# A hybrid encoder layer on one core: equal matmul widths side by side, W cleared in pieces, two heads' inverses sent apart

## The chip, the core and the metric

The kernel runs on one core of a Trainium2 chip. TensorE (PE) does the matmuls, VectorE (DVE) and ScalarE (ACT) the elementwise work, GpSimd (POOL) clears memory and issues part of the DMAs, SyncE (SP) issues the others. The metric is the device time of one execution in microseconds; before the change its median over three runs is 2288.46 us (2286.44 to 2289.66).

## The reference, cut to what matters

Two sequences of 256 tokens (width 2048) go through one encoder layer and a last RMSNorm. All arithmetic is float32.

```
proj  = rmsnorm(h) @ w_in
y_na  = neighbourhood_attention(q, k, v, rpb)         # 8 heads; 4 rows of 64 columns, windows of 16 columns
y_dn  = gated_deltanet_bidir(qkv, z, b, a, ...)       # 8 heads; forwards and backwards, chunks of 64 tokens
h     = h + concat(y_na, y_dn) @ w_out
hn    = rmsnorm(h)
h     = h + (silu(hn @ w_gate) * (hn @ w_up)) @ w_down
# within a chunk of the delta rule:
a_mat = strict lower part of (k_beta @ k.T) * decay
t_mat = inverse of (I + a_mat)                        # triangular, 64 x 64
u = t_mat @ v_beta;  w = t_mat @ (k_beta * exp(g));  then a recurrence over 4 chunks
```

## The kernel before

Every float32 product is made of products in the fp32r format. A weight tile of 128x1024 is split by `split` (L135, L136): ACT writes its rounded part `w_hi`, DVE the remainder `w_lo`. Activations are kept as such pairs too.

The stages, by time in the trace:

- To about 230 us: the q and k column tiles of the delta-rule heads (`col_tile`, each two `half_gemm` of 24 matmuls, 512 columns wide), the convolution, Gram matrices sent to DRAM (`s_gram`).
- 230 to 520 us: the q, k, v tiles of the eight attention heads; beside them runs `attend` (L615) as a generator that `pump` advances between matmuls. At the same time `lanes` (L477) inverts all 128 chunk matrices at once, one per partition, on DVE: `W` (128 partitions x 64 x 64, in the buffer that held the decays `E`) is cleared by one POOL memset (L552), then filled column by column (L562, L564); `half_gemm` advances this generator once per half tile. The results are written over `kkq` (L574 for partitions 0 to 63, L577 for 64 to 127) and sent to DRAM (`s_uq`, L582) by eight DMAs of 16 partitions on POOL's queue.
- 520 to 780 us: v and z tiles of the delta-rule heads, and beside them the recurrence. `open_recurrence` opens the pool `dr` in the memory that `lanes` gave back, clears the four buffers `uq` (L703) and `prepare` reads the inverses of a head back from `s_uq` (L720, four DMAs a head, POOL's queue). The matmul that needs them is `ps_s<-dvn,uq`.
- 780 to 950 us: the output projection (`w_out`).
- 950 to 1815 us: gate and up. 44 calls of `block` compute a 2x2 block product with seven products instead of eight (sums of weights come from accumulating DMAs and DVE). 1858 to 2177 us: 16 such blocks of the down projection, in two groups of eight; the rest of it (`down`, `down_half`) is plain.

One call of `product` (L985) is 8 matmuls of 512 columns with `w_hi` (7 in the down groups), then 8 (7) of 256 columns with `w_lo`. The scheduler keeps the matmuls in the order of the program. Other engines' instructions are ordered by a planner from priorities (`tc.high_priority`) and due times; each engine then runs its instructions in that order. Weight splits go through three buffers each for `hi` and `lo`.

In `attend`, the score rows `na_s` (tags `s0`, `s1`) hold probabilities and zeros outside the window: each head takes new tiles and POOL clears the outside (L636); the output `na_o` takes the buffer `s0` and is sent to `s_na` by POOL's queue (L674).

Of the kernel before, what the change touches and what calls it, by code (L numbers as in the profile page):

```python
# [18 lines left out]
P = 128  # L19
# [36 lines left out]
FIN_GAP = 5  # L56

LANE_WORK = 1800
HALF, BAND = 32, 40

WARM = 56
# [10 lines left out]
def hybrid_encoder(ctx: ExitStack, tc: tile.TileContext, xT, w_in, w_ba, w_out, w_gate,  # L72
# [50 lines left out]
    s_qq = dp.tile([4, H, NB, C], F32, name="s_qq")  # L123
    s_kq = dp.tile([H, P, 2, T], F32, name="s_kq")
    s_gram = dp.tile([4, H * NB, C, 2, C], F32, name="s_gram")
    s_uq = dp.tile([H * NB, 2, C, 4, 2, C], F32, name="s_uq")
    s_na = dp.tile([H, P, T], F32, name="s_na")
    s_h1 = dp.tile([KT, P, T], F32, name="s_h1")
    s_h2 = dp.tile([KT, P, T], F32, name="s_h2")
# [338 lines left out]
    def decays(s0, s1):  # L468

        G, NG, E = gt["G"], gt["NG"], gt["E"]  # L470
        for s in range(s0, s1):
# [2 lines left out]
            pin(act(out=E[half[1], s, :s + 1], in_=G[half[1], :s + 1], func=AF.Exp,  # L474
                    bias=NG[half[1], s:s + 1]))

    def lanes():  # L477
        beta, kd, eg, dg, E = (gt[n] for n in ("beta", "kd", "eg", "dg", "E"))
        qq = vec("qq")

        gram = s_gram.rearrange("k n s w c -> (k n) s (w c)")
        quarters = [slice(q * 16, q * 16 + 16) for q in range(4)]
        for sl in quarters:
            nc.gpsimd.dma_start(kkq[half[0], sl].rearrange("p s w c -> p s (w c)"), gram[:, sl])
        for d in range(2):
            nc.gpsimd.dma_start(qq[half[d]], s_qq.rearrange("k h b t -> (k h b) t"))
        yield from pause(LANE_START)
        for q, sl in enumerate(quarters):
            pin(nc.scalar.copy(kkq[half[1], sl], kkq[half[0], sl]))
            if q % 2:  # L490
                yield


        def norms(src, nm):
            x, s, r = vec(nm + "x"), vec(nm + "s"), vec(nm + "r")
            pin(ts(x, src, EPS, None, ALU.add))
            newton_rsqrt(r, x, ln)
            tt(s, x, r, ALU.mult)
            return s, r

        dgk = kkq.rearrange("p s w c -> p (s w c)")[:, 0:C * 2 * C:2 * C + 1]
        nk, rk = norms(dgk, "nk")
        _, rq = norms(qq, "nq")
        yield
        rqd = vec("rqd", 2 * C)
        for i in range(2):
            ts(rqd[:, i * C:i * C + C], rq, QSCALE, None, ALU.mult)
        egd = vec("egd", 4 * C)
        for i in range(2):
            stt(egd[:, i * C:i * C + C], eg, -1.0, rk, ALU.mult, ALU.mult)  # L510
            nc.vector.tensor_copy(egd[:, (2 + i) * C:(3 + i) * C], eg)
        Dm, ndm, rb = vec("Dm"), vec("ndm"), vec("rb")
        tt(rb, rk, beta, ALU.mult)
        tt(Dm, rk, rb, ALU.mult)
        ts(ndm, Dm, -1.0, None, ALU.mult)
        yield

        LN = {(0, 0): 0, (0, 1): 16, (0, 2): 64 + 16, (0, 3): 64,
              (1, 0): 64 + 48, (1, 1): 64 + 32, (1, 2): 32, (1, 3): 48}
        for q in range(2):  # L520
            sl = slice(q * 32, q * 32 + 32)
            tt(kkq[:, sl, 1], kkq[:, sl, 1], E[:, sl], ALU.mult)
            yield

        h0, h1 = half
        Et = E[h0].rearrange("p s c -> p c s")
        for q in range(4):
            sl = slice(q * 16, q * 16 + 16)
            n = q * 16 + 16
            tt(kkq[h0, sl, 0, :n], kkq[h0, sl, 0, :n], Et[:, sl, :n], ALU.mult)  # L530
            tt(kkq[h1, sl, 0, :n], kkq[h1, sl, 0, :n], E[h1, sl, :n], ALU.mult)
            tt(kkq[:, sl, 0, :n], kkq[:, sl, 0, :n], ndm[:, sl, None].broadcast_to([P, 16, n]),
               ALU.mult)
            yield
        ps = sm_tile()
        mm(ps[:, :P], ones, dg, start=True, stop=True)
        nc.scalar.copy(egl, ps[:, :P])
        ps = sm_tile()
        for i, v in enumerate((kd, egd[:, :2 * C], egd[:, 2 * C:], rqd)):
            transpose(ps[:, i * P:i * P + P], v, ident)  # L540
        p3 = ps[:, :3 * P].rearrange("p (i l) -> p i l", i=3)
        for (hf, st), l0 in LN.items():
            nc.scalar.copy(tab[half[hf], :, st], p3[half[hf], :, l0:l0 + 16])
        for hf in range(2):
            for pp in range(2):
                l0 = 3 * P + POS[pp][hf] * 16
                nc.scalar.copy(rqs[half[hf], pp], ps[half[hf], l0:l0 + 16])
        yield

        W = ln.tile([P, C, C], F32, tag="E", name="W")  # L550
        Wf = W.rearrange("p s c -> p (s c)")
        nc.gpsimd.memset(W, 0.0)  # L552
        nc.vector.memset(Wf[half[0], 0:C * C:C + 1], 1.0)
        nc.vector.tensor_copy(Wf[half[1], 0:C * C:C + 1], Dm[half[1]])
        work = 0
        for c in range(1, C):
            for s0 in range(0, c, BLK):
                s1 = min(s0 + BLK, c)
                n, j = s1 - s0, c - s0
                pr = ln.tile([P, BLK * C], F32, tag="prod", bufs=2, name="prod")  # L560
                pv = pr[:, :n * j].rearrange("p (s j) -> p s j", j=j)
                tt(pv, W[:, s0:s1, s0:c], kkq[:, c, 0, None, s0:c].broadcast_to([P, n, j]),  # L562
                   ALU.mult)
                nc.vector.tensor_reduce(W[:, s0:s1, c], pv, AX.X, ALU.add)  # L564
                work += 2 * n * j + 200
            if work > LANE_WORK:
                work = 0
                yield

        for d in range(2):  # L570
            for q in range(2):
                sl = slice(q * 32, q * 32 + 32)
                if d == 0:
                    tt(kkq[h0, sl, 0], W[h0, sl], rb[h0, sl, None].broadcast_to([64, 32, C]),  # L574
                       ALU.mult)
                else:
                    tt(kkq[h1, sl, 0], W[h1, :, sl].rearrange("p s c -> p c s"),  # L577
                       nk[h1, sl, None].broadcast_to([64, 32, C]), ALU.mult)
                yield
            for (hf, st), l0 in LN.items():  # L580
                if l0 // 64 == d:
                    nc.gpsimd.dma_start(  # L582
                        s_uq[:, hf, :, st].rearrange("n s w c -> n s (w c)"),
                        kkq[l0:l0 + 16].rearrange("p s w c -> p s (w c)"))

    for h in range(H):
        kq = wk.tile([P, 2, T], F32, tag="kq", bufs=2, name="kq")
# [24 lines left out]
    def part(s, c0, shift, n):  # L612
# [2 lines left out]
        return bass.AP(a.tensor, a.offset,  # L615
                       [a.ap[0], (L + shift * (C - BAND if shift > 0 else BAND), 2), (C, 4), (1, n)])

    def attend(h, qT, kT, v):

        bias = na.tile([P, 2, 4 * BAND], F32, tag="bias", bufs=2, name="bias")  # L620
# [9 lines left out]
                   by_rows(kT, b)[:, :, k0:k0 + BAND], start=True, stop=True)  # L630
        sc = []
        for b in range(NB):
            full = na.tile([P, 2, L], F32, tag=f"s{b}", name="na_s")
            sc.append(full)
            s = part(full, 0, 1, BAND)
            nc.gpsimd.memset(part(full, BAND, -1, C - BAND), 0.0)  # L636
            tt(s, pq[b][:, :8 * BAND].rearrange("p (q r c) -> p q r c", q=2, r=4),
               bias.rearrange("p q (r c) -> p q r c", r=4), ALU.add)
            mx = na.tile([P, 2], F32, tag="mx", bufs=2, name="mx")
# [24 lines left out]
            nc.scalar.copy(t, pt.rearrange("p (q k) -> p q k", q=2))  # L664
            pT.append(t)
        yield from pause(PV_GAP)
        no = na.tile([P, T], F32, tag="s0", name="na_o")
        po = sm_tile()
        for b in range(NB):
            for kt in range(2):  # L670
                mm(po[:, b * L:b * L + L], vn[:, b * 2 + kt], pT[b][:, kt],
                   start=(kt == 0), stop=(kt == 1))
        nc.scalar.copy(no, po)
        nc.gpsimd.dma_start(s_na[h], no)  # L674

    for h in range(H):
        ps = col_tile(w_in[16 + 3 * h], xs)
# [29 lines left out]

    prepared, outputs, gate, traced, finished = {}, {}, {}, set(), set()

    def prepare(h, vT):  # L710

        dr, UQ = state["dr"], state["UQ"]
        while h > 1 and not {h - 2, h - 2 ^ 1} <= traced:
            yield
        uq = UQ[2 * (h % 2):2 * (h % 2) + 2]
        kq = wk.tile([P, 2, T], F32, tag="kq", bufs=2, name="kq2")
        nc.sync.dma_start(kq, s_kq[h])
        for b in range(NB):
            for hf in range(2):
                nc.gpsimd.dma_start(  # L720
                    uq[b][half[hf], :, :, hf * C:hf * C + C].rearrange("s i w c -> s (i w) c"),
                    s_uq[h * NB + b, hf].rearrange("s i w c -> s (i w) c"))
        yield from pause(2 + h % 2)
        pv, pk = sm_tile(), sm_tile()
        for t, u in ((pv, vT), (pk, kq[:, 0])):
# [140 lines left out]
    for h in range(0, H, 2):  # L866
        vT = []
        for i in range(2):
            if h + i == 1:
                while vector_work:  # L870
                    advance(vector_work)
            while h and h + i - 2 not in prepared:
                pump()
            ps = col_tile(w_in[40 + 2 * (h + i)], xs)
# [107 lines left out]

    def product(ps, w, xc, c, first, done=False):  # L985

        wh, wl = w
        for k, x in enumerate(xc):
            mm(ps, wh[:, k], x[:, c], start=(first and k == 0), stop=False,
               skip_group_check=True)  # L990
        for k, x in enumerate(xc):
            mm(ps[:, 0], wl[:, k], x[:, c, 0], start=False, stop=(done and k == len(xc) - 1),
               skip_group_check=True)

    def plus_both(out, a, ps, op=ALU.add):
# [33 lines left out]
    def block(w4, sums, xc, ix, p1_pool, new_out, opened=None, lead=False):  # L1029
# [15 lines left out]
        pc, pd = bank(psm, "s", "ps_c"), bank(pso, "o1", "ps_d")  # L1045
        with ahead():
            w = w_split(b11)
        product(pa, w, xc, ix[A11], True)
        if lead:
            pe = bank(psm, "s", "ps_e")  # L1050
            with ahead():
                w = w_split(b21)
            product(pe, w, xc, ix[A12], True, True)
        if opened:
            opened()
        fp, out = state["fp"], new_out()
# [3 lines left out]
            plus_both(out[:, 0], p1, pe)  # L1060
        with ahead():
            w = w_split(second)
        product(pc, w, xc, ix[S3], True)
        p7 = fp.tile([P, 2, L], F32, tag="p7", name="p7")
        nc.scalar.copy(p7, pc)
        with ahead():
# [321 lines left out]
```

## Time and profile before

The median is 2288.46 us. The profiled execution took 2286.66 us by the device's own clock, its span is 2284.9 us.

| engine | busy us | share of the span | instructions |
|---|---|---|---|
| PE | 2251.9 | 99% | 12318 |
| DVE | 1760.5 | 77% | 2691 |
| ACT | 1058.2 | 46% | 1637 |
| POOL | 246.2 | 11% | 358 |

The granted TensorE clock is 0.997 of full speed over the span. A matmul row shows when it began and how long it took with its drain, which overlaps the next one; so the pace of the matmuls is read from one start to the next, not from their durations, and a PE that is 99% busy can still have slack in its pace. In a row of the timeline stand start, duration, engine, line, operation, output<-inputs, shapes, count and, in brackets, the engine's idle time before it and what ended it.

### The profile page before, as it was taken

The numbers are of one execution on the slowest core, as the hardware profiler recorded it, in microseconds if no ns is written. First come the engines' busy times: TensorE is split into PE (matmuls) and PEld (weight loads), VectorE is DVE, ScalarE is ACT, GpSimd is POOL, SyncE is SP. The second block draws the span as 40 slices with busy tenths as digits, with TensorE's granted clock in tenths as the row PEclk, the third lists the DMA queues.
The fourth block names the chain that finished last, engine by engine and source line by source line (L and its number), as shares of the span: only waits on it lengthen the run. The fifth ranks groups of instructions, "written<-read, shape, count | busy, mean of one in ns | idle before, by whom it ended". The sixth has DMA issues, their size and how long they took to land.

```text
span 2284.9 us, 32561 instructions
## 1 busy us (share of the span) xinstructions
PE 2251.9 (99%) x12318; PEld 1920.3 (84%) x12318; DVE 1760.5 (77%) x2691; ACT 1058.2 (46%) x1637; POOL 246.2 (11%) x358
## 2 busy tenths in 40 slices
PE   9999999999999999999999999999999999999998
PEld 7887788887888888888888888888888878888887
DVE  7754699983555545888888888888888788888866
ACT  6777332324333324654444444444444454444435
POOL 2211100011000010111111010101010011011110
PEclk9999999999999999999999999999999999999999
DMA  5333423245333454776777677777777477667672
GB/s 203 128 127 126 129 84 104 95 125 148 109 98 107 176 175 166 218 204 183 216 199 206 193 213 202 205 198 205 197 187 202 143 209 200 173 189 210 182 203 84
DMA packets 112316, 383.95 MB, mean 168 GB/s; under 512 B 14080, under 2 KB 14416, under 8 KB 111904
## 3 DMA queue, kind: packets, MB, share of 16 engines
q1 hardware_dynamic: 77264, 267.17, 33.5%
q0 software_dynamic: 34896, 114.71, 23.8%
q8 instruction: 97, 1.59, 0.3%
q14 instruction: 59, 0.48, 0.1%
HBM read 346.41 MB, written 35.41 MB: 167 GB/s over the span
## 4 chain that ended last, share of the span: by engine, by line
PE 83%; DVE 7%; ACT 4%; issue 3%; DMA 2%; POOL 0%; SPq 0%; DVEq 0%; ACTq 0%; POOLq 0%
PE ps_g L84 28%; PE ps_c L84 14%; PE ps_d L84 14%; PE ps_a L84 14%; PE ps_b L84 7%; PE ps_s L84 6%; DVE w_lo L136 2%; ACT w_hi L135 1%; DVE cacc L351 1%; ACT E L472 1%; ACT E L474 1%; PE ps_o L84 1%; PE ps_s L87 1%; DMA kkq<-s_gram 1%; DVE W L564 0%
## 5 line engine op out<-in xcount | busy, mean ns | idle before, releaser
L84 PE MATMUL ps_g<-xhi,w_hi 128*128 128x512 f32 x896 | 359.0, 401 | 2.7 <-DVE on L442 1.4
L84 PE MATMUL ps_g<-xhi,w_lo 128*128 128x512 f32 x896 | 351.4, 392 | 5.7 <-DVE w_lo L136 5.7
L84 PE MATMUL ps_g<-xlo,w_hi 128*128 128x512 f32 x896 | 350.2, 391 | 0.5 <-DVE xlo L255 0.5
L135 ACT ACTIVATE w_hi<-w_first 128x1024 fp32r<-128x1024 f32 (+1 forms) x180 | 185.7, 1032 | 285.9 <-PE ps_c L84 157.2
L136 DVE TENSOR_TENSOR w_lo<-w_raw,w_hi 128x1024 fp32r<-128x1024 f32 x166 | 202.4, 1220 | 133.1 <-ACT w_hi L135 132.7
L135 ACT ACTIVATE w_hi<-b 128x1024 fp32r<-128x1024 f32 (+1 forms) x180 | 185.7, 1032 | 227.9 <-issue 122.6
L135 ACT ACTIVATE w_hi<-w_raw 128x1024 fp32r<-128x1024 f32 x166 | 174.3, 1055 | 243.2 <-PE ps_g L84 201.8
L136 DVE TENSOR_TENSOR w_lo<-w_first,w_hi 128x1024 fp32r<-128x1024 f32 (+1 forms) x180 | 213.4, 1185 | 50.4 <-ACT w_hi L135 45.6
L136 DVE TENSOR_TENSOR w_lo<-b,w_hi 128x1024 fp32r<-128x1024 f32 (+1 forms) x180 | 212.7, 1182 | 3.8 <-ACT w_hi L135 3.2
L84 PEld LDWEIGHTS ps_g<-xhi,w_lo 128*128 128x128 f32 x896 | 168.7, 188 | 44.5 <-DVE w_lo L136 8.4
L84 PEld LDWEIGHTS ps_g<-xhi,w_hi 128*128 128x128 f32 x896 | 168.8, 188 | 39.9 <-issue 4.5
L84 PEld LDWEIGHTS ps_g<-xlo,w_hi 128*128 128x128 f32 x896 | 168.9, 188 | 35.1 <-DVE xlo L255 1.5
L84 PE MATMUL ps_c<-xc,w_hi 128*128 128x512 f32 x704 | 176.3, 392 | 0.0
L84 PE MATMUL ps_d<-xc,w_hi 128*128 128x512 f32 x704 | 176.3, 392 | 0.0
L84 PE MATMUL ps_a<-xc,w_hi 128*128 128x512 f32 x696 | 174.2, 392 | 0.0
L84 PEld LDWEIGHTS ps_c<-xc,w_hi 128*128 128x128 f32 x704 | 126.6, 189 | 22.6
L84 PEld LDWEIGHTS ps_d<-xc,w_hi 128*128 128x128 f32 x704 | 126.6, 189 | 22.6
L84 PEld LDWEIGHTS ps_a<-xc,w_hi 128*128 128x128 f32 x696 | 125.2, 189 | 22.4
L135 ACT ACTIVATE w_hi<-w_second 128x1024 fp32r<-128x1024 f32 (+1 forms) x60 | 61.9, 1032 | 94.4 <-PE ps_d L84 85.5
L84 PEld LDWEIGHTS ps_d<-xc,w_lo 128*128 128x128 f32 x704 | 96.0, 190 | 6.9
L84 PEld LDWEIGHTS ps_c<-xc,w_lo 128*128 128x128 f32 x704 | 96.0, 190 | 6.9
L84 PEld LDWEIGHTS ps_a<-xc,w_lo 128*128 128x128 f32 x696 | 94.9, 190 | 6.8
(374 smaller groups left out, 4223.0 us busy)
## 6 DMA issues: line engine op xcount, KB each, us to landing
w_raw<-in_w_in_dram SPq DMA_DIRECT2D x110, 512.0 KB, 3.2
b<-in_w_gate_dram SPq DMA_DIRECT2D x66, 512.0 KB, 3.9
b<-in_w_up_dram SPq DMA_DIRECT2D x66, 512.0 KB, 4.7
b<-in_w_group_dram SPq DMA_DIRECT2D x48, 448.0 KB, 4.1
w_raw<-in_w_out_dram SPq DMA_DIRECT2D x32, 512.0 KB, 3.4
w_raw<-in_w_down_dram SPq DMA_DIRECT2D x24, 512.0 KB, 3.4
w_second<-in_w_gate_dram SPq DMA_DIRECT2D x22, 512.0 KB, 7.4
w_first<-in_w_gate_dram SPq DMA_DIRECT2D x22, 512.0 KB, 5.8
```

The costliest lines, as they stand in the source:

```text
L84: pin(nc.tensor.matmul(*a, **k))
L87: pin(nc.tensor.transpose(*a))
L135: act(out=hi, in_=src, func=AF.Copy)
L136: tt(lo, src, r32(hi), ALU.subtract)
L351: stt(a3[:, :, lo:hi], x3[:, :, lo + o:hi + o], cw[:, ct, j:j + 1], a3[:, :, lo:hi], ALU.mult, ALU.add)
L472: pin(act(out=E[half[0], s, s:], in_=G[half[0], s:], func=AF.Exp, bias=NG[half[0], s:s + 1]))
L474: pin(act(out=E[half[1], s, :s + 1], in_=G[half[1], :s + 1], func=AF.Exp, bias=NG[half[1], s:s + 1]))
```

## The change

- `product` writes wide matmuls first and narrow ones second in one call, and the other way round in the next, so that runs of equal width adjoin across calls; `plain` (the leading block of a stage) starts the count anew with wide first. The flag that begins an accumulation moves to the first matmul of the call, whichever it is.
- `W` is cleared by eight memsets that cover, for each group of eight rows, only the columns up to the diagonal block: 2304 of 4096 elements per partition.
- The two probability tiles are taken once, and their outside is cleared once. `na_o` takes the buffer `vT` and is sent by ACT's DMA queue.
- `s_uq` becomes two DRAM tiles: one for heads 0 and 1 (4 of each group of 16 lanes), one for heads 2 to 7 (12). `send_lanes` sends the first part as soon as each half of the inverses is done, the second part after both: 16 DMAs instead of 8, the same bytes.
- The remaining vector work is drained, the recurrence memory opened and the fetch for heads 0 and 1 (`fetch`) issued before the first v tile, where before the drain stood before the second v tile, and opening and fetch after it.

In the built program PE's instructions stand in the old order up to the first leading block, SP's up to the second down group. On POOL's queue the clears of `uq` and the fetch follow directly behind the 16 pieces of `s_uq`; the sends of `na_o` no longer stand between them. On ACT and DVE some instructions of `attend` and of the blocks change places with weight splits.

```diff
+OPEN_AT = 0
-    s_uq = dp.tile([H * NB, 2, C, 4, 2, C], F32, name="s_uq")
+    s_uq = [dp.tile([n, 2, C, 4, 2, C], F32, name=f"s_uq{n}") for n in (4, 12)]
...
+    def send_lanes(part, d):
+        n0, n1 = ((0, 4), (4, 16))[part]
+        for (hf, st), l0 in LN.items():
+            if l0 // 64 == d:
+                nc.gpsimd.dma_start(
+                    s_uq[part][:, hf, :, st].rearrange("n s w c -> n s (w c)"),
+                    kkq[l0 + n0:l0 + n1].rearrange("p s w c -> p s (w c)"))
...
-        nc.gpsimd.memset(W, 0.0)
+        for s in range(0, C, 8):
+            nc.gpsimd.memset(W[:, s:s + 8, :s + 8], 0.0)
...
-            for (hf, st), l0 in LN.items():
-                if l0 // 64 == d:
-                    nc.gpsimd.dma_start(
-                        s_uq[:, hf, :, st].rearrange("n s w c -> n s (w c)"),
-                        kkq[l0:l0 + 16].rearrange("p s w c -> p s (w c)"))
+            send_lanes(0, d)
+        send_lanes(1, 0)
+        send_lanes(1, 1)
...
-            full = na.tile([P, 2, L], F32, tag=f"s{b}", name="na_s")
-            sc.append(full)
-            s = part(full, 0, 1, BAND)
-            nc.gpsimd.memset(part(full, BAND, -1, C - BAND), 0.0)
+            if b not in probs:
+                probs[b] = na.tile([P, 2, L], F32, tag=f"s{b}", name="na_s")
+                nc.gpsimd.memset(part(probs[b], BAND, -1, C - BAND), 0.0)
+            sc.append(probs[b])
+            s = part(probs[b], 0, 1, BAND)
...
-        no = na.tile([P, T], F32, tag="s0", name="na_o")
+        no = na.tile([P, T], F32, tag="vT", name="na_o")
...
-        nc.gpsimd.dma_start(s_na[h], no)
+        nc.scalar.dma_start(s_na[h], no)
...
+    def fetch(h):
+        uq = state["UQ"][2 * (h % 2):2 * (h % 2) + 2]
+        kq = wk.tile([P, 2, T], F32, tag="kq", bufs=2, name="kq2")
+        nc.sync.dma_start(kq, s_kq[h])
+        for b in range(NB):
+            for hf in range(2):
+                nc.gpsimd.dma_start(
+                    uq[b][half[hf], :, :, hf * C:hf * C + C].rearrange("s i w c -> s (i w) c"),
+                    s_uq[h > 1][(h * NB + b) - 4 * (h > 1), hf].rearrange("s i w c -> s (i w) c"))
+        fetched[h] = uq, kq
...
     def prepare(h, vT):
...
+        if h not in fetched:
+            fetch(h)
+        uq, kq = fetched[h]
...
-            if h + i == 1:
+            if h + i == OPEN_AT:
                 while vector_work:
                     advance(vector_work)
+                open_recurrence()
+                fetch(0)
+                fetch(1)
...
-    def product(ps, w, xc, c, first, done=False):
+    def product(ps, w, xc, c, first, done=False, plain=False):
         wh, wl = w
-        for k, x in enumerate(xc):
-            mm(ps, wh[:, k], x[:, c], start=(first and k == 0), stop=False,
-               skip_group_check=True)
-        for k, x in enumerate(xc):
-            mm(ps[:, 0], wl[:, k], x[:, c, 0], start=False, stop=(done and k == len(xc) - 1),
+        n = len(xc)
+        wide = [(ps, wh[:, k], x[:, c]) for k, x in enumerate(xc)]
+        narrow = [(ps[:, 0], wl[:, k], x[:, c, 0]) for k, x in enumerate(xc)]
+        if plain:
+            order[0] = 0
+        work = narrow + wide if order[0] % 2 else wide + narrow
+        order[0] += 1
+        for m, (out, w, x) in enumerate(work):
+            mm(out, w, x, start=(first and m == 0), stop=(done and m == 2 * n - 1),
                skip_group_check=True)
...
-        product(pa, w, xc, ix[A11], True)
+        product(pa, w, xc, ix[A11], True, plain=lead)
...
-            product(pe, w, xc, ix[A12], True, True)
+            product(pe, w, xc, ix[A12], True, True, plain=True)
...
-        product(pc, w, xc, ix[S3], True)
+        product(pc, w, xc, ix[S3], True, plain=lead)
```

More of the change, by code (lines that the diff above doesn't have):

```diff
@@ L475, in decays @@
                     bias=NG[half[1], s:s + 1]))
+    LN = {(0, 0): 0, (0, 1): 16, (0, 2): 64 + 16, (0, 3): 64,
+          (1, 0): 64 + 48, (1, 1): 64 + 32, (1, 2): 32, (1, 3): 48}
+    def send_lanes(part, d):
[5 more added lines that the diff above has]
+                    kkq[l0 + n0:l0 + n1].rearrange("p s w c -> p s (w c)"))
     def lanes():
@@ L516, in lanes @@
         yield
-        LN = {(0, 0): 0, (0, 1): 16, (0, 2): 64 + 16, (0, 3): 64,
-              (1, 0): 64 + 48, (1, 1): 64 + 32, (1, 2): 32, (1, 3): 48}
         for q in range(2):
@@ L616, in part @@
                        [a.ap[0], (L + shift * (C - BAND if shift > 0 else BAND), 2), (C, 4), (1, n)])
+    probs = {}
     def attend(h, qT, kT, v):
@@ L708, in hybrid_encoder @@
     prepared, outputs, gate, traced, finished = {}, {}, {}, set(), set()
[L710 to L715, printed above, removed]
+    fetched = {}
+    def fetch(h):
+        uq = state["UQ"][2 * (h % 2):2 * (h % 2) + 2]
         kq = wk.tile([P, 2, T], F32, tag="kq", bufs=2, name="kq2")
@@ L721, in prepare @@
                     uq[b][half[hf], :, :, hf * C:hf * C + C].rearrange("s i w c -> s (i w) c"),
-                    s_uq[h * NB + b, hf].rearrange("s i w c -> s (i w) c"))
+                    s_uq[h > 1][(h * NB + b) - 4 * (h > 1), hf].rearrange("s i w c -> s (i w) c"))
+        fetched[h] = uq, kq
+    def prepare(h, vT):
+        dr = state["dr"]
+        while h > 1 and not {h - 2, h - 2 ^ 1} <= traced:
+            yield
+        if h not in fetched:
+            fetch(h)
+        uq, kq = fetched[h]
         yield from pause(2 + h % 2)
@@ L980, in hybrid_encoder @@
             tt(acc, acc, sq, ALU.add)
-    def product(ps, w, xc, c, first, done=False):
+    order = [0]
+    def product(ps, w, xc, c, first, done=False, plain=False):
         wh, wl = w
-        for k, x in enumerate(xc):
-            mm(ps, wh[:, k], x[:, c], start=(first and k == 0), stop=False,
-               skip_group_check=True)
-        for k, x in enumerate(xc):
-            mm(ps[:, 0], wl[:, k], x[:, c, 0], start=False, stop=(done and k == len(xc) - 1),
+        n = len(xc)
[7 more added lines that the diff above has]
+            mm(out, w, x, start=(first and m == 0), stop=(done and m == 2 * n - 1),
                skip_group_check=True)
```

## Prediction

> **What bounds the kernel now.** I read the page's busy shares and chain first, then the waits of PE, then the timeline at the places that the change touches.
>
> ```profile
> span 2284.9 us, 32561 instructions
> PE 2251.9 (99%) x12318; PEld 1920.3 (84%) x12318; DVE 1760.5 (77%) x2691; ACT 1058.2 (46%) x1637; POOL 246.2 (11%) x358
> PE 83%; DVE 7%; ACT 4%; issue 3%; DMA 2%; POOL 0%; SPq 0%; DVEq 0%; ACTq 0%; POOLq 0%
> PE ps_g L84 <- DVE w_lo L136: 6.5, 5, 3.9
> PE ps_s L84 <- DMA uq<-s_uq: 3.2, 2, 2.5
> ```
>
> PE is busy all the time and carries 83% of the chain, so two things alone can shorten the run: matmuls that follow each other faster, and the few waits of PE. Of these the two longest kinds are shown: 6.5 us for `w_lo`, 3.9 of it at one place, and 3.2 us for the inverses coming back. The change reaches the pace, the 3.9 and the 3.2. DVE, ACT and POOL matter only through what PE waits for.
>
> **Runs of one width.** The first fence holds six products of the gate stage, the second two matmuls 52 places apart in the output projection (wide only, across half-tile boundaries) and a run of 86 narrow ones near the end.
>
> ```profile
> 1501.78 2.00 PE L84 MATMUL ps_a<-xc,w_hi 128*128 128x512 f32 x8
> 1503.62 1.12 PE L84 MATMUL ps_a<-xc,w_lo 128*128 128x256 f32 x8
> 1504.57 2.00 PE L84 MATMUL ps_c<-xc,w_hi 128*128 128x512 f32 x8
> ...
> 1518.54 0.63 PE L84 MATMUL ps_c<-xc,w_hi 128*128 128x512 f32 x2
> ```
>
> ```profile
> 830.00 0.39 PE L84 MATMUL ps_g<-nmh,w_lo 128*128 128x512 f32 x1
> ...
> 841.79 0.39 PE L84 MATMUL ps_g<-nmh,w_hi 128*128 128x512 f32 x1
> ...
> 2239.80 10.48 PE L84 MATMUL ps_g<-aq,wd 128*128 128x256 f32 x86
> ```
>
> A product takes (1518.54 - 1501.78)/6 = 2.793 us from start to start. Undisturbed, a wide matmul takes (841.79 - 830.00)/52 = 0.2267, a narrow one (10.48 - 1.12)/(86 - 8) = 0.120 (eight of them take 1.12 with the drain). Eight and eight make 1.814 + 0.960 = 2.774. So one turn from narrow to wide and back costs 0.0195 us: the wide run loses 0.026 (1.84 instead of 1.814), the narrow one gains 0.01 (0.95). The wide-only run crosses two half tiles, with new weights and waits, at an even 0.2267, so it is the width and not the beginning of a product that costs. The 420 calls had 420 turns to narrow and 416 to wide; alternating, with the two leading blocks kept plain, leaves 213 of each: some 205 pairs go, 205 x 0.0195 = **4.0 us**. Bounds 3.6 to 4.4 from the rounding; nothing if the cause is another (below).
>
> The price could be paid back by waits, since a narrow-first product needs `w_lo` at its start, 1.84 us sooner. In the steady stage that is covered:
>
> ```profile
> 1513.35 1.23 DVE L136 TENSOR_TENSOR w_lo<-w_first,w_hi 128x1024 fp32r<-128x1024 f32 x1 [0.36 <-ACT w_hi L135]
> ```
>
> This `w_lo` is the one of the product at 1518.54: done at 1514.58, 3.96 us ahead of the product's start. The new order of DVE puts up to four short evacuations or one 1.2 us product ahead of a split, which eats at most 1.6; a narrow-first product also gives back its `hi` buffer 0.95 later, which delays the split three products on by as much. 3.96 - 1.6 - 0.95 leaves 1.4. I take nothing. In the leading block of the down groups there is no cover:
>
> ```profile
> 1866.91 1.09 DVE L136 TENSOR_TENSOR w_lo<-w_first,w_hi 128x896 fp32r<-128x896 f32 x1 [1.83 <-ACT w_hi L135]
> 1866.93 1.90 PE L84 MATMUL ps_d<-xd,w_hi 128*128 128x512 f32 x7 [0.55 <-ACT w_hi L135]
> 1870.43 1.88 PE L84 MATMUL ps_b<-xd,w_hi 128*128 128x512 f32 x7 [0.76 <-ACT w_hi L135]
> 1874.25 0.93 PE L84 MATMUL ps_d<-xd,w_hi 128*128 128x512 f32 x3 [1.11 <-DVE p L1071]
> ```
>
> There `ps_d` becomes narrow-first and begins at 1868.05 instead of 1866.93. But it then runs through in about 2.45, `ps_b` begins at about 1870.5 instead of 1870.43, and the wait at 1874.25 is set by DVE's own chain, not by PE: the 1.1 us disappear there. Nothing, twice.
>
> **W in pieces.**
>
> ```profile
> 259.00 0.26 POOL L636 MEMSET na_s<- 128x192 f32 x1 [11.18 <-DVE kkq L522]
> 271.55 3.52 POOL L552 MEMSET W<- 128x4096 f32 x1 [12.28 <-DVE kkq L531]
> 271.92 3.19 DVE L496 TENSOR_SCALAR nqx<-qq 128x64 f32<-128x64 f32 x1
> 275.26 0.22 DVE L510 SCALAR_TENSOR_TENSOR egd<-eg,nkr 128x64 f32<-128x64 f32 x1
> 275.90 1.22 DVE L136 TENSOR_TENSOR w_lo<-w_raw,w_hi 128x1024 fp32r<-128x1024 f32 x1
> 277.17 0.80 PE L84 MATMUL ps_g<-xhi,w_lo 128*128 128x512 f32 x1 [3.85 <-DVE w_lo L136]
> ```
>
> A 64-element DVE instruction lasts 3.19 us and ends with POOL's clear of `W` (271.55 + 3.52 = 275.07); others of its size take about 0.2. Everything behind it on DVE is 2.9 to 3.0 late, the `w_lo` at 275.90 among it, and PE stands 3.85 us. From 192 elements in 0.26 and 4096 in 3.52 a clear costs 0.10 plus 0.00084 per element: the eight pieces, 2304 elements, take 2.7 in all, the longest 0.53. If DVE gets in behind the running piece, it and two more such instructions behind it lose about 0.9 together and some 2.2 are saved; if POOL keeps DVE out until the last piece, 3.52 - 2.7 = 0.8; if it loses nothing, 2.9. I take **2.2**, since the stall ends with the instruction that holds POOL, and the pieces are instructions of their own. The column recursion behind moves forward with PE. The clears of `na_s` that go (14 of 0.26) hide beside PE: nothing.
>
> **The fetch.**
>
> ```profile
> 494.57 0.79 POOL L582 DMA_DIRECT2D s_uq<-kkq  x1 [29.02 <-DVE kkq L574]
> 496.02 3.82 DVE L577 TENSOR_TENSOR kkq<-W,nks 64x2048 f32<-64x2048 f32 x1
> 508.54 3.02 POOL L582 DMA_DIRECT2D s_uq<-kkq  x4 [1.52 <-issue]
> 536.72 0.57 POOL L674 DMA_DIRECT2D s_na<-na_o  x1 [25.15 <-ACT na_o L673]
> 537.28 3.65 POOL L703 MEMSET uq<- 128x1024 f32 x4
> 540.86 5.42 POOL L720 DMA_DIRECT2D uq<-s_uq  x8
> 546.93 0.60 PE L84 MATMUL ps_s<-dvn,uq 128*128 128x128 f32 x4
> 550.02 0.46 PE L84 MATMUL ps_s<-dvn,uq 128*128 128x128 f32 x2 [2.48 <-DMA uq<-s_uq]
> 551.16 0.46 PE L84 MATMUL ps_s<-dvn,uq 128*128 128x128 f32 x2 [0.68 <-DMA uq<-s_uq]
> s_uq<-kkq POOLq DMA_DIRECT2D x8, 512.0 KB, 16.7
> uq<-s_uq POOLq DMA_DIRECT2D x32, 128.0 KB, 3.3
> ```
>
> POOL's queue stood 25.15 us behind the send of the last `na_o`; only then came the clears (3.65), eight fetches (5.42) and their landing, and PE lost 2.48 + 0.68 = 3.16. That send now goes to ACT. The first four pieces follow 494.57; those of the other half wait for L577, done at 499.84; at most 0.79 each, the last piece is issued by about 509.3, the clears end at 513, the fetches are issued by 518.4. They read behind pieces still in flight: a 512 KB send landed 16.7 us after issue, so 509.3 + 16.7 + 3.3 = 529, or 532 with 5.42 for eight instead of 3.3. Needed at 546.93, less the 2.2 by which both sides move. The wait goes: **3.2 us** (bounds 1.6, if only half goes, and 3.2). Nothing else is late there: the next rows of PE wait for no one.
>
> ACT's eight sends have no row: nothing to 0.57 each (POOL's above), on an ACT that is 46% busy. Each stands before a split, and a whole 0.57 would reach PE only where that split has no cover. I take nothing, up to 0.5 in all.
>
> **What moves against it.** On ACT the order around the softmax changes, and one split per attention head has no cover:
>
> ```profile
> 405.94 0.87 DVE L640 TENSOR_REDUCE mx<-na_s 128x2 f32<-128x320 f32 x2
> 407.75 0.41 ACT L643 ACTIVATE na_s<-na_s,mx 128x160 f32<-128x160 f32 x1
> 408.16 1.05 ACT L135 ACTIVATE w_hi<-w_raw 128x1024 fp32r<-128x1024 f32 x1
> 409.95 1.21 DVE L136 TENSOR_TENSOR w_lo<-w_raw,w_hi 128x1024 fp32r<-128x1024 f32 x1
> 411.22 0.49 PE L84 MATMUL ps_g<-xhi,w_lo 128*128 128x512 f32 x1
> ```
>
> `w_lo` ends at 411.16, PE takes it at 411.22. The second maximum of this head ended at 406.81. In the new order 1.95 us more of the column recursion stand ahead of it on DVE (the durations of the moved rows summed), so it ends near 408.76; two exponentials of 0.41 stand behind it and ahead of this `w_hi`, which begins near 409.6, ends at 410.65 and lets `w_lo` begin 0.7 late. In the other heads the shifts are 0.3 or less, some backwards. I take **+0.7** (bounds -0.5 and +2.5, the latter 0.5 for each of five heads).
>
> Sum: -4.0 - 2.2 - 3.2 + 0.7 = -8.7 us, against the profiled execution's 2286.66: 2278.0. That execution lies 1.8 under the median 2288.46, within the spread of the runs; from the median it is 2279.8. I forecast **2279.0**.
>
> **Rivals.** (a) The turn of width costs nothing in itself; what I measured belongs to the start of a product and stays. Then 2286.66 - 2.2 - 3.2 + 0.7 = 2282.0. The even wide-only run speaks against it. [...] Chance 0.10.
>
> (b) The attention stage gives the gains back: DVE is in arrears there, and if each of six heads loses 1.0 more at its tight split, 2278.0 - 0.7 + 6.0 = 2283.3. For it: zero cover in the rows above. Against it: shifts that large stand in one head. Chance 0.08.
>
> (c) Slower: the pieces. A send of 4 or 12 partitions may use only 4 or 12 DMA engines; if they are always the same ones, the busiest carry 16 shares where they carried eight. The old stream ran from 494.57 to about 511.56 + 16.7 = 528; twice its 33.7 ends at 562, and eight fetches behind it (5.42 + 3.3) at 571: PE stands 26 instead of 3.2, 2286.66 - 4.0 - 2.2 + 0.7 + 23 = 2304. It decides as soon as the pieces land after about 536. [...] No row here shows which engines a send uses. Chance 0.05. Other losses, such as splits late for narrow-first products: 0.02.
>
> **How the numbers follow.** Forecast 0.75, (a) 0.10, (b) 0.08, (c) and others 0.07. The smallest gain of the likeliest case is 3.6 + 0.8 + 1.6 - 2.5 - 0.5 = 3.0, the largest 4.4 + 2.9 + 3.2 + 0.5 = 11.0; from the slowest run 2289.66 and the fastest 2286.44 that is 2286.7 down to 2275.4. Range 2275.4 to 2286.7, which takes in (a) and (b). 0.2%, about what a measurement of this kernel can tell from no change, is 4.6 us: (b), half of (a) and a tenth of the forecast fall within. Faster 0.78, same 0.15, slower 0.07.
>
> **What would show it.** Right: a period of two products of 5.57 instead of 5.587; no DVE instruction of 64 elements over 0.8 near 272; PE's wait at 277 down to about 1.6; no wait of PE for `uq`. Wrong: waits of PE for `w_lo` in the gate stage, products still at 2.793, `uq` landing after 544, or DVE held from the first to the last piece.

## The result and the profile after

The changed kernel is slower by 0.3%: 2293.74 us median (2291.63 to 2295.48) against 2287.2 (2284.87 to 2289.66), ratio 1.0027, 95% interval 1.0016 to 1.0038. Its profiled execution took 2294.59 us. The forecast was 2279.0.

The page of the changed kernel (span, busy shares, shares of the chain):

```profile
span 2292.8 us, 32540 instructions
PE 2251.9 (98%) x12318; PEld 1922.5 (84%) x12318; DVE 1768.2 (77%) x2691; ACT 1059.6 (46%) x1637; POOL 244.1 (11%) x351
PE 77%; DVE 11%; ACT 5%; DMA 4%; issue 3%; POOL 0%; SPq 0%; DVEq 0%; ACTq 0%; POOLq 0%
```

PE does the same work in the same busy time, but it has less of the chain, and DMA has twice its share (4% for 2%). The waits of PE (who waited for whom: us in total, times, longest):

```profile
PE ps_s L85 <- ACT pT L677: 6.5, 1, 6.5
PE ps_s L88 <- ACT dvT L356: 4.0, 3, 2.8
...
PE ps_s L88 <- ACT dvn L751: 3.6, 1, 3.6
PE ps_s L85 <- DVE kT L697: 2.2, 2, 1.9
```

The wait for `uq` is gone and the long one for `w_lo` too. Four others stand in their place: for `pT` (the transposed probabilities of the last attention head), `dvT` and `dvn` (the v tile of a delta-rule head after its convolution, and its transposed copy) and `kT` (the k tile of an attention head). Where the time went shows when the starts of the 12318 matmuls are set side by side, each counted in its order. Number 1500 begins 4.8 us sooner than before (318.2 against 323.0), number 2400 3.2 sooner (515.7 against 518.9), number 2600 11.1 later (571.7 against 560.6), number 4600, in the output projection, still 11.1, number 12000 7.5. So 14.3 us are lost between 516 and 572 us, and the 3.7 that come back lie in the gate and down stages.

What happens in that stretch (timeline of the changed kernel: start, duration, engine, line, in brackets the idle time before and what ended it):

```profile
516.02 0.80 POOL L486 DMA_DIRECT2D s_uq<-kkq  x1 [8.34 <-DMA s_uq<-kkq]
521.21 1.07 ACT L136 ACTIVATE w_hi<-w_raw 128x1024 fp32r<-128x1024 f32 x1 [9.68 <-DMA w_raw<-in_w_in_dram]
528.39 1.06 ACT L136 ACTIVATE w_hi<-w_raw 128x1024 fp32r<-128x1024 f32 x1 [6.11 <-DMA w_raw<-in_w_in_dram]
529.48 1.23 DVE L137 TENSOR_TENSOR w_lo<-w_raw,w_hi 128x1024 fp32r<-128x1024 f32 x1 [5.35 <-ACT w_hi L136]
533.80 1.28 ACT L356 ACT_TABLE_LOAD   x1 [3.27 <-DVE cacc L352]
...
536.67 1.05 ACT L677 COPY pT<-ps_s 128x512 f32<-128x512 f32 x2
537.28 3.78 PE L85 MATMUL ps_s<-pT,vn 128*128 128x256 f32 x8 [6.48 <-ACT pT L677]
...
544.95 1.06 ACT L136 ACTIVATE w_hi<-w_raw 128x1024 fp32r<-128x1024 f32 x1 [7.23 <-DMA w_raw<-in_w_in_dram]
550.78 0.85 PE L88 MATMUL ps_s<-ident,dvT 128*128 128x128 f32 x4 [2.76 <-ACT dvT L356]
554.59 0.58 ACT L751 COPY dvn<-ps_s 128x512 f32<-128x512 f32 x1 [3.55 <-DMA s_na<-na_o]
555.22 1.12 PE L88 MATMUL ps_s<-ident,kq 128*128 128x128 f32 x4 [3.59 <-ACT dvn L751]
```

ACT stands and waits for weights to land, and what is behind the split waits with it. For `dvT` (PE at 550.78) that is the split at 544.95. For `pT` there are more steps: the split at 528.39 is late, DVE's half of it (529.48) and the convolution `cacc` behind that are late, ACT waits 3.27 us for `cacc`, and `pT` stands behind that on ACT. The engine named in PE's waits is ACT; the cause is further back, in the brackets of ACT and DVE. The chain of work that ended last says the same for 500 to 565 us: 68% of it are these two landings, 11.4% the send of `na_o` for which `dvn` waits, and in the kernel before weights have no share of it.

```profile
498.20 22.92 DMA w_raw<-in_w_in_dram
...
523.56 21.30 DMA w_raw<-in_w_in_dram
```

DMA issues of 494 to 562 us (count, size, median us to landing), the changed kernel and then the kernel before:

```profile
w_raw<-in_w_in_dram SPq DMA_DIRECT2D x9, 512.0 KB, 18.4
s_uq<-kkq POOLq DMA_DIRECT2D x8, 384.0 KB, 28.4
uq<-s_uq POOLq DMA_DIRECT2D x8, 128.0 KB, 17.0
s_uq<-kkq POOLq DMA_DIRECT2D x4, 128.0 KB, 19.9
s_na<-na_o ACTq DMA_DIRECT2D x2, 256.0 KB, 10.1
```

```profile
w_raw<-in_w_in_dram SPq DMA_DIRECT2D x11, 512.0 KB, 9.4
s_uq<-kkq POOLq DMA_DIRECT2D x8, 512.0 KB, 16.7
...
```

A weight took 9.4 us to land here before, which the buffers ahead of the splits cover (PE has no wait for it), and takes 18.4 now, which they don't. The same stretch in one row (window, PE busy, PEld, DVE, ACT, POOL, granted clock, mean busy share of the 16 DMA engines, GB/s), before and after:

```profile
485.00:560.00 75.00, 71.84 (x358) 60.03 (x357) 40.32 (x48) 26.22 (x47) 16.77 (x24) 1.00 0.65 169
```

```profile
485.00:560.00 75.00, 62.17 (x277) 50.94 (x276) 33.39 (x39) 21.52 (x38) 22.09 (x28) 0.91 0.80 155
```

The DMA engines are busier (0.80 for 0.65) and move less (155 GB/s for 169). This is the row on which the experiments turn.

### The profile page after: what moved, and what is told of

The parts are those of the page before. It is cut to its first block, busy times and chain, and to the rows that moved or that the text cites. A ratio compares the mean times of both kernels' runs of the same rounds, so it can differ in the third digit from the quotient of the medians.

```text
span 2292.8 us, 32540 instructions
## 1 busy us (share of the span) xinstructions
PE 2251.9 (98%) x12318; PEld 1922.5 (84%) x12318; DVE 1768.2 (77%) x2691; ACT 1059.6 (46%) x1637; POOL 244.1 (11%) x351
## 4 chain that ended last, share of the span: by engine, by line
PE 77%; DVE 11%; ACT 5%; DMA 4%; issue 3%; POOL 0%; SPq 0%; DVEq 0%; ACTq 0%; POOLq 0%
PE ps_g L85 23%; PE ps_d L85 14%; PE ps_c L85 14%; PE ps_a L85 13%; PE ps_b L85 7%; PE ps_s L85 5%; DVE w_lo L137 3%; DMA w_raw<-in_w_in_dram 2%; DVE W L576 1%; DVE prod L574 1%; ACT w_hi L136 1%; DVE cacc L352 1%; ACT E L473 1%; DMA w_first<-in_w_group_dram 1%; ACT E L475 1%
## 5 line engine op out<-in xcount | busy, mean ns | idle before, releaser
L85 PE MATMUL ps_d<-xc,w_lo 128*128 128x256 f32 x704 | 98.5, 283 | 0.0
L85 PE MATMUL ps_c<-xc,w_lo 128*128 128x256 f32 x704 | 98.5, 283 | 0.0
L85 PE MATMUL ps_a<-xc,w_lo 128*128 128x256 f32 x696 | 97.4, 283 | 0.0
```

Of the source, the lines that this page charges most:

```text
L85: pin(nc.tensor.matmul(*a, **k))
```

## Experiments

There are three theories. **P**: the pieces of 4 and 12 lanes hold the DMA engines longer than whole sends, and the weights come late. **F**: the early fetch stands in the way. **N**: the send of `na_o` from ACT, out of the buffer `vT`, holds up `dvn`, which takes that buffer next. All were timed in five rounds beside the kernel before.

**Whole sends in the changed kernel.**

```diff
-        n0, n1 = ((0, 4), (4, 16))[part]
-                    s_uq[part][:, hf, :, st]..., kkq[l0 + n0:l0 + n1]...
+                    s_uq[:, hf, :, st]...,       kkq[l0:l0 + 16]...
```

> The changed kernel with the inverses sent in eight sends of 16 lanes as before; all else as changed. Theory P (the pieces: a send of 4 lanes keeps only 4 DMA engines busy and two such sends share a way into SBUF, so its 4096-byte packets take 1.25 us instead of 0.73; the stream of the inverses fills the DMA engines longer and the weights come late): PE's waits of 6.5, 2.8 and 3.6 us near 530 to 555 go, the 14.3 us lost between 516 and 560 come back, time about 2279.5. Theory F (the early fetch stands in the way, whatever the size of the sends): the waits stay, at least 2289. Theory N (na_o in the buffer vT, sent from ACT): at most 3.6 us change, at least 2290.

2281.3 us (ratio 0.9973, 0.9963 to 0.9983): 12.4 less than the changed kernel. Its row of the stretch and the longest wait left in it:

```profile
485.00:560.00 75.00, 72.88 (x377) 60.71 (x377) 36.81 (x44) 26.19 (x47) 15.18 (x20) 0.98 0.63 161
```

```profile
PE ps_s L88 <- ACT dvn L748: 2.1, 1, 2.1
```

P holds; the 6.5 and the 2.8 are gone, with the fetch still called early.

**Pieces alone, in the kernel before.** `s_uq`, `send_lanes` and its calls as in the changed kernel, nothing else.

> The kernel before with one part of the change: the inverses sent in pieces of 4 and 12 lanes, in the changed order; the fetch stays where it was, behind the last na_o on POOL. Theory P: the weights come late here too, PE loses 10 us or more between 516 and 560, time 2297 to 2304. Theories F and N: nothing new stands in the way, 2287, at most 1 more for a later uq.

2296.83 us (1.0045, 1.0032 to 1.0057): 10.3 slower, just under what P expected, DMA engines 0.73 busy in the stretch. The pieces do it by themselves. F falls with these two.

**The last `na_o` in `s0`**, first with whole sends, then with the pieces. (A buffer of its own for `na_o` does not fit: the pool would need 34.59 kb per partition, and 34.5 are left.)

```diff
-        no = na.tile([P, T], F32, tag="vT", name="na_o")
+        no = na.tile([P, T], F32, tag="s0" if h == H - 1 else "vT", name="na_o")
```

> The changed kernel with whole sends, and the last head's na_o in the buffer s0 instead of vT, so that the copy dvn has no send of ACT's to wait for. Theory P with N as its smaller part: the 2.1 us wait for dvn that the whole sends had left goes, 2281.3 becomes 2279.2. If the DMA engines are what dvn's successors wait for as well, another wait takes its place and the time stays at 2281.

> The changed kernel, pieces and all, with the last head's na_o in the buffer s0 instead of vT. Theory P: the 3.6 us that dvn waited for ACT's send go there, but the weights are as late: 2289 to 2293. Theory N (that wait is the cause): 2282 or less.

With whole sends 2277.3 us (0.9962, 0.9949 to 0.9974): 4.0 less, more than the 2.1 expected, which agrees with the matmuls behind that stop having run at a lower clock too (0.98 granted over the stretch, 1.00 without the stop). With the pieces 2291.51 (1.0015, 1.0006 to 1.0024): dvn's wait goes, and these stand (waits of PE):

```profile
PE ps_s L85 <- ACT pT L677: 5.0, 1, 5.0
...
PE ps_s L85 <- DMA uq<-s_uq: 3.2, 3, 1.5
```

So N is a second, smaller cost, and most of it is covered while the weights and the inverses are late.

**The fetch at its old place**, on whole sends and `s0`: `OPEN_AT = 1`, the two calls of `fetch` taken out.

> Whole sends and the last na_o in s0 (2277.3), with the fetch of the first two heads put back to its old place behind dvT of head 1. If the fetch had to be called sooner for PE not to wait: uq lands late again, 3.2 us more, 2280.5. If moving the send of na_o from POOL to ACT was enough by itself: 2277.

2277.27 us (0.9961, 0.9948 to 0.9973), the same as with the early fetch. POOL issues the fetch from 523.90 to 533.84 here and from 524.07 in the run with whole sends alone, where it was called early: in both as soon as the inverses have landed; what had held it before was the send of `na_o` on POOL's queue, and moving that send was enough. PE's row of the stretch has no gap left:

```profile
485.00:560.00 75.00, 75.00 (x400) 62.92 (x400) 38.21 (x47) 28.03 (x52) 15.17 (x20) 1.00 0.67 169
```

**Why pieces are slow: 8 lanes, and another order.** In the changed kernel the first sends carry lanes 0 to 3, 16 to 19, 32 to 35 and 48 to 51. The trace's packet records show 4 packets under way while one such send is alone, 0.73 us each of 4096 bytes, and 16 under way at 1.25 us when four are in flight. A whole send in the kernel before alone has 14 to 16 under way on the mean as well (496 to 500 us), at 0.73 us each, so the number under way is not what makes them slow. A window in which each kernel has the DMA engines full of these sends, before (whole) and after:

```profile
496.50:500.00 3.50, 3.50 (x17) 2.99 (x16) 3.47 (x2) 1.65 (x2) 0.17 (x1) 1.00 0.98 88
```

```profile
496.50:500.00 3.50, 3.50 (x17) 2.89 (x16) 1.68 (x2) 0.00 (x0) 1.77 (x4) 1.00 0.92 55
```

The same engines move 55 GB/s instead of 88, and by the packet records only 42 of the 55 are packets of these sends; the rest are weights. My guess was that some of the sends in flight meet on one way at SBUF (the expectations call it a way into SBUF); in the changed kernel lanes 0 to 3 and 32 to 35 are in flight together. The records give the packets' times and show no such way: it is a guess.

> The changed kernel with the pieces cut at 8 lanes instead of 4: sixteen sends of 8 lanes. Theory P in its form 'engines as many as lanes, packets slow only where sends in flight share a way into SBUF': two sends in flight fill 16 engines, packets take 0.73 us as in whole sends, and the time is near that of the whole sends, about 2280. Theory P in its form 'the fewer lanes, the slower': packets of 0.9 to 1.25 us, 2290 or more. Theories F and N: as the changed kernel, 2294.

Pieces of 8 lanes (`((0, 8), (8, 16))[part]`): 2293.53 us (1.0033, 1.0021 to 1.0045), the DMA engines 0.77 busy. My reading, that two sends in flight fill the engines and nothing meets, falls: packets took 0.86 to 1.15 us from 495 to 499 us, and 0.73 to 0.77 only from 500 to 504. Lanes 0 to 7 and 32 to 39 are in flight together all the same (POOL issues the first four sends from 490.05 to 493.30); that these two slow each other is argued and not shown. The other form, the fewer lanes the slower, forecast this time too. The next run keeps the pieces and changes their order:

```diff
-            send_lanes(0, d)
-        send_lanes(1, 0)
-        send_lanes(1, 1)
+        send_lanes(0)
+        send_lanes(1)
...
+        for l0 in (0, 64, 16, 80, 32, 96, 48, 112):
```

> The changed kernel with its sixteen pieces sent in another order, all behind the last product of the inverses: lanes 0, 64, 16, 80, 32, 96, 48, 112 instead of 0, 16, 32, 48 and then the upper half. If the pieces are slow because sends in flight meet on one way into SBUF (in the changed kernel lanes 0 to 3 and 32 to 35 were in flight together and packets took 1.25 us): packets of the 4-lane sends take 0.73 us, the stream holds the DMA engines as long as whole sends do (441 us over all engines instead of 638), time 2280 to 2284. If it is the number of lanes alone, or the eight sends that POOL can have open: 2291 to 2296.

The order alone: 2284.65 us (0.9997, 0.9988 to 1.0005), 9.1 less than the changed kernel, with the same sixteen sends of 4 and 12 lanes; the guess had let expect 2280 to 2284, the other readings 2291 and more. Stretch and longest wait:

```profile
485.00:560.00 75.00, 69.88 (x341) 58.33 (x340) 35.76 (x41) 25.38 (x46) 22.00 (x28) 0.95 0.65 162
```

```profile
PE ps_s L88 <- ACT dvn L750: 5.1, 1, 5.1
```

The share is back at 0.65. The packets tell it more exactly: 1280 packets of 4096 bytes on POOL's queue from 480 to 580 us took 644 us together in the changed kernel, 633 in the pieces of 8 lanes, 441 with whole sends and 440 in this order (475 in the next run, which has this order too). So the slow packets come with the order of the sends, and not with the number of lanes. (What is behind that is not shown: the order changes which sends are in flight together, and also which addresses in DRAM are written side by side; no run here separates the two.) What is left:

> The pieces in the order that keeps sends in flight apart (2284.7), with the last head's na_o in s0. If the waits of dvn (5.1 us) was all that the pieces still cost: 2277.5 to 2280. If the pieces hold the weights up as well: 2282 or more.

2284.1 us (0.9989, 0.9981 to 0.9998), hardly less: with dvn's wait gone, `uq` is late.

```profile
PE ps_s L85 <- DMA uq<-s_uq: 4.3, 3, 1.8
```

From the first issue to the last landing of the inverses, by the trace, it takes 37.9 us with whole sends (with `s0`), 53.7 in this order and 64.0 in the changed kernel. In the changed kernel each send from the ninth on begins 0.28 to 0.62 us after the one eight places ahead of it has landed (the row at 516.02 above, 8.34 us idle; the send eight places ahead landed at 515.74), and the fetch queues behind. Which share of the 16 us between 37.9 and 53.7 is due to that, and which to sends of fewer lanes with fewer packets under way (4 for one of 4 lanes alone), is not settled. In time, the order is between half and three quarters of what the pieces cost: with `na_o` in `vT` the pieces cost 12.4 us and the order gives 9.1 back, with the last one in `s0` they cost 14.2 and it gives 7.4 back.

**Turns of width.** First the alternation alone in the kernel before, then each product in four runs:

> The kernel before with one part of the change: products alternate wide first and narrow first, the leading blocks plain. If a turn of width costs, as forecast: 4.0 us less, 2282.5, of which the waits of ps_d for w_lo in the down groups may take 0.3 to 0.7 back. If a start of a product costs and not the turn: 2286.5.

2282.99 us (0.9988, 0.9979 to 0.9997): 3.5 less. In its profile matmul 12000 has gained 4.1 on matmul 4600.

```diff
+        work = wide[:4] + narrow[:4] + wide[4:] + narrow[4:]
```

> The kernel before with each product cut into four runs: four wide, four narrow, the other wide ones, the other narrow ones. The work is the same, the turns of width double: 420 pairs more. If a pair of turns costs 0.0195 us: 8.2 us more, 2294.7. If the start of a product costs: 2286.5. A wait for w_lo, needed 0.9 us sooner with 3.96 us in hand, should not show.

2291.15 us (1.002, 1.0011 to 1.003): 4.7 more, so the turn costs and not the start of a product, but a turn in runs of four costs less than one in runs of eight. Starts of products (timeline):

```profile
1500.65 1.09 PE L84 MATMUL ps_c<-xc,w_hi 128*128 128x512 f32 x4
...
1509.07 1.09 PE L84 MATMUL ps_d<-xc,w_hi 128*128 128x512 f32 x4
```

8.42 us for three products, 2.807 each instead of 2.793. The loss is in the first five wide matmuls behind a turn (233, 236, 228, 232 and 231 ns apart instead of 227), and runs of four end before the fifth. Why a turn costs, no run here shows.

**W.** First its pieces alone in the kernel before:

> The kernel before with one part of the change: W cleared in eight pieces. Forecast of the prediction: 2.2 us less, 2284.3. Theory of the clock (behind PE's stop of 4.2 us ten matmuls stand 0.427 us apart instead of 0.227, 2 us that the prediction did not count): the stop falls to about 1.4 and the slow matmuls go with it, 4 to 5 us less, 2281.5 to 2282.5, less what a later wait takes back.

2297.14 us (1.0046, 1.0033 to 1.0059): 10.6 slower, which neither theory had. POOL and PE in that run:

```profile
509.51 0.26 POOL L637 MEMSET na_s<- 128x192 f32 x1 [9.22 <-DMA s_na<-na_o]
```

```profile
530.95 1.22 PE L87 MATMUL ps_s<-ident,na_s 128*128 128x128 f32 x4 [5.70 <-ACT na_s L648]
535.60 0.63 PE L84 MATMUL ps_g<-xhi,w_lo 128*128 128x512 f32 x1
```

The inverses were ready 2.4 us sooner, and two whole sends of them, instead of one, got ahead of the last-but-one `na_o`. It landed 10.6 us after issue instead of 5.1, and the clear of the last head's probabilities in the same buffer `s0` waited for it, and the softmax behind the clear. Behind the stop the matmuls are at half pace (0.63 us with the drain at 535.60, 0.39 before it; 0.43 from start to start instead of 0.23).

```diff
+        (W in pieces, as above)
-        no = na.tile([P, T], F32, tag="s0", name="na_o")
+        no = na.tile([P, T], F32, tag="s0" if h == H - 1 else "vT", name="na_o")
```

> The kernel before with W cleared in pieces, and na_o of all heads but the last in vT instead of s0 (still sent from POOL). Reading of the run with W alone (2297.1): the clear of the last head's probabilities in s0 waited 9.2 us for the send of na_o out of s0, which had got behind three sends of inverses. By it the 5.7 us wait and the slow matmuls behind it go, 2284 to 2287. If W in pieces costs the 10 us in another way: 2296.

2285.4 us (0.9997, 0.9988 to 1.0006): the reading holds. Last, W whole again inside the version without the collision (whole sends, the last `na_o` in `s0`, late fetch):

> The version with whole sends, the last na_o in s0 and the late fetch (2277.3), with W cleared in one instruction again. Prediction's term: 2.2 us more, 2279.5. Theory of arrears (what the pieces give PE at 272 it pays back by waits for kT, 3.5 us in three places, because DVE is behind): within 1 us of 2277.3. With the ten slow matmuls behind PE's 4.2 us stop counted: 4 us more less the kT waits, 2278 to 2280.

2279.48 us (0.9967, 0.9955 to 0.998): 2.2 more than 2277.27, 2.5 when each is set against the kernel before of its own rounds. Its waits and, below, those of the version with pieces:

```profile
PE ps_g L85 <- DVE w_lo L137: 6.3, 5, 4.0
```

```profile
PE ps_g L85 <- DVE w_lo L137: 3.8, 6, 1.1
PE ps_s L85 <- DVE kT L694: 2.2, 2, 1.9
```

## Why the prediction was wrong

The sum was right for another kernel. It said -8.7 us; the version with whole sends, `na_o` of the last head in `s0` and every other edit is 9.2 below the kernel before it was timed with (2277.3 against 2286.5). That it comes so close is in part luck, as W and the fetch show. Term by term:

- **Runs of one width, -4.0**: right. Alone -3.5; in the changed kernel -3.7 from matmul 4600 to 12000. The period of two products is the 5.57 that was asked for (timeline of the changed kernel, two narrow-first products):

```profile
1502.66 1.12 PE L85 MATMUL ps_b<-xc,w_lo 128*128 128x256 f32 x8
1503.62 2.00 PE L85 MATMUL ps_b<-xc,w_hi 128*128 128x512 f32 x8
...
1508.23 1.12 PE L85 MATMUL ps_c<-xc,w_lo 128*128 128x256 f32 x8
```

  "Nothing, twice" held at both places. In the down group PE does wait for `w_lo` (1.83 us at 1875.77), and matmul 9840 and 10060, on either side of it, are 8.1 and 8.0 behind. Rival (a) falls.
- **W in pieces, -2.2**: the right size from wrong parts. No 64-element instruction waits any more:

```profile
269.83 2.43 POOL L564 MEMSET W<- 128x64 f32 x8 [23.35 <-DVE kkq L542]
...
270.15 0.22 DVE L509 TENSOR_SCALAR nqx<-qq 128x64 f32<-128x64 f32 x1
```

  PE's stop falls from 3.85 to 1.08. The prediction overlooked a second price of that stop, which the profile of before shows: the matmuls behind it start 0.43 us apart instead of 0.227.

```profile
277.76 0.63 PE L84 MATMUL ps_g<-xhi,w_hi 128*128 128x512 f32 x1
278.19 0.63 PE L84 MATMUL ps_g<-xlo,w_hi 128*128 128x512 f32 x1
```

```profile
270.00:284.00 14.00, 10.15 (x36) 7.84 (x35) 13.78 (x36) 1.06 (x1) 4.27 (x3) 0.76 0.17 59
```

  The granted clock of this window is 0.76 (1.00 in the changed kernel); some ten matmuls lose 2 us. Against it "The column recursion behind moves forward with PE" was wrong: DVE has a backlog there, the stop had let it catch up, and without the stop PE waits for `kT` instead: 2.2 us in two waits, and shorter ones. The two errors cancel. A single profile does not size this better than to 2 us: the two runs whose edits touch nothing before 950 us (alternation alone, runs of four) reach matmul 1500 by 0.2 and 2.0 us sooner than before.
- **The softmax, +0.7**: not resolved. With W whole, PE loses 0.4 us from matmul 1500 to 2100 against before, but the run with the alternation alone, whose edit touches nothing there, gains 1.0 in the same stretch. Rival (b), with 6.0 us, falls.
- **The fetch, -3.2**: it came, 3.7 from matmul 2400 to 2700 in the version without the collision, but from the send of `na_o` that left POOL's queue, not from the early call.
- **The step that failed** stands in the fetch: "a 512 KB send landed 16.7 us after issue, so 509.3 + 16.7 + 3.3 = 529", and behind it "Nothing else is late there: the next rows of PE wait for no one". The landing time of a whole send was put on pieces whose packets take 1.25 us instead of 0.73 when four are in flight, with POOL taken to issue them without waiting; the last piece was issued at 520.68 instead of 509.3 and landed at 553.9. And "no one" looked only at what PE waited for in the profile of before, not at the weights, which go over the same 16 DMA engines and already needed 9.4 us there instead of the 3.2 of the whole run.

Rival (c), chance 0.05, had the place and the sign: its condition, pieces that land after about 536, was met. Its mechanism was another, the same few engines for every send; with four sends of 4 lanes in flight 16 packets are under way and the 16 engines are 0.92 busy (496.5 to 500 us), so the sends do spread over the engines, with packets that take 1.25 us each. Its price was too high (+23 where the stretch lost 14.3 net) and its victim wrong: PE never waited for `uq`, because ACT's late weights held it up first.

## What to carry to other kernels

Price a DMA together with its neighbours in flight, and not by its bytes alone: here the same 1280 packets took 644 us in one order of sixteen sends and 440 in another. When a transfer is cut up or moved, look up every other transfer in that stretch and how much later it may land; the profile's time to landing in the window (9.4 us against 3.2 over the whole run) told that the stretch had little left. A buffer shared between a send and a later write ties the compute order to the DMA queue's load: the same edit of W gave +10.6 us alone, no measurable difference with that buffer changed, and -2.2 in the version without the collision.

## What the runs showed of the hardware

Some stops of PE cost more than their length. Behind those of 3.85 us (before, from 273.3) and 6.48 us (changed kernel, from 530.8) the granted clock was 0.50 for 6.83 us (276.22 to 283.04 and 535.34 to 542.17), and the matmuls of 512 columns in it started 0.43 us apart instead of 0.227. A stop of 1.83 us at the head of the first down group of the changed kernel was followed by seven such matmuls (the row shows 7 in 3.12 us with the drain, where the product `ps_c` before the stop has 1.89).

```profile
1875.77 1.10 PE L85 MATMUL ps_d<-xd,w_lo 128*128 128x256 f32 x7 [1.83 <-DVE w_lo L137]
1876.70 3.12 PE L85 MATMUL ps_d<-xd,w_hi 128*128 128x512 f32 x7
```

A longer stop need not do this: in the kernel before PE stands 2.48 us for `uq` from 547.53 to 550.02 (and 0.68 up to 551.16), and the clock stays at 1.00. The clock records of the two traces agree with one reading. In both the granted clock moves between 1.00 and 0.50 alone, and in each all its changes lie whole multiples of 3.413 us apart (before: 2 and 584 of them; changed kernel: 2, 3, 2, 386, 1 and 118), as if it were set anew at each step of a fixed grid. Two windows of that grid in the changed kernel (columns as above, the granted clock third from the end):

```profile
1873.37:1876.78 3.41, 1.58 (x13) 1.38 (x13) 2.16 (x3) 1.42 (x2) 0.86 (x1) 1.00 0.92 242
1876.78:1880.19 3.41, 3.41 (x10) 2.65 (x9) 2.33 (x4) 1.79 (x2) 0.86 (x1) 0.50 0.65 107
```

Here the whole stop lies in one window (PE busy 1.58 of 3.41 us), and the next one runs at half clock. In the kernel before a boundary of its grid, 549.28, falls into the stop of 2.48 us: its two windows have 1.74 and 1.42 us idle, and neither the second nor the one behind it runs at half clock:

```profile
545.87:549.28 3.41, 1.67 (x10) 1.28 (x8) 0.00 (x0) 0.37 (x1) 0.41 (x1) 1.00 0.98 245
549.28:552.70 3.42, 2.00 (x10) 1.64 (x11) 0.00 (x0) 0.37 (x1) 0.00 (x0) 1.00 0.07 14
552.70:556.11 3.41, 3.41 (x30) 2.72 (x29) 1.92 (x2) 2.62 (x6) 0.00 (x0) 1.00 0.00 0
```

Over these two traces every window at full clock in which PE stood for 1.83 us or more was followed by one at half clock (six windows: 2.90 and 2.14 us before, 1.83, 2.56, 2.58 and 3.41 us in the changed kernel), and none in which it stood for 1.74 or less.
